# A fifth pair of gates in seven products, block sums in raw tiles of their own, and new deals of the pieces

## The chip, the core and the metric

The kernel runs on one core of one Trainium2 chip. The metric is the device time of one launch in microseconds (us), as the median of several runs. Five engines work side by side: PE (matrix products), DVE and ACT (elementwise work), POOL and SP (here mostly transfers). SP issues nearly all loads of weights. Products are accumulated in PSUM, which has eight banks; everything else lies in SBUF.

## The reference

One decoder block on 256 tokens of width 2048, in float32. Every matrix product below is a float32 product to the accuracy of a split into two parts.

```python
proj = einsum('bsd,de->bse', rmsnorm(x, mix_norm_w), w_in)
(q, k, v, g_out, gk_low, gate_b, gate_c, xc, merge_a, merge_b) = split(proj)
o = rmsnorm(gla_chunked(q, k, v, log_g), gla_norm_w)
y_a = o * silu(g_out)
y_b = gate_b * causal_depthwise_conv(gate_c * xc, conv_w)
merged = sigmoid(merge_a) * y_a + sigmoid(merge_b) * y_b
h = x + merged @ w_out
gu = rmsnorm(h, ffn_norm_w) @ w_gate_up
h = h + (silu(gate) * up) @ w_down
return rmsnorm(h, final_norm_w)
```

## The kernel before

**Pieces.** The weights (some 290 MB) are read once and a little more, in pieces of 128 x 1024 values, 512 KB. A piece goes through four stations: SP issues its load into a buffer `raw`; ACT rounds it into `hi` (`high`, L265); DVE writes the rest into `lo` (`low`, L270); PE multiplies. Each product is three matmuls (`mm3`, L374 to L376): activations hi with weights lo, activations lo with weights hi, hi with hi. There are 5 buffers `raw`, 6 `hi` and 5 `lo`, and `take` loads up to 5 pieces ahead of the one in use. `lo` of a piece is formed one piece later than its `hi` (`halfway`, `finish_low`).

**Eights and sevens.** A group of 512 columns (for instance g3, the third block of `g_out`) is used in one of two ways. As *eights*, it has 8 pieces with 12 matmuls each: two chunks of the contracted dimension, two halves of the tokens. Two groups can also be taken as a *pair in sevens*, by a scheme with seven block products in place of eight: the pair then has 28 pieces of 6 matmuls. In each of four quads q the pieces are `11` (a loaded piece, kept in a buffer y), `t1`, `t3`, `t2`, `t4` (sums of loaded pieces, formed by DVE in `sum_of`), and after the quads come eight pieces `21` and `22`, loaded once more. A pair adds up in five banks, called _0 to _4 after the pair's first key: _0 takes `11` and `21`, _1 takes `t1` and `22`, _2 `t2`, _3 `t3`, _4 `t4`. When the quads are over, DVE combines the banks; bank _1 must be read (`u = pb + v3`) before the `22` pieces may be added on it, and the result goes to a tile that `second` allocates.

**Sums.** `t1` = y + x goes to a `raw` buffer. `t3`, `t2` and `t4` are formed one after the other in place in x, so that each must be split into `hi` and `lo` before the next one overwrites it; `sum_of` calls `finish_low` for that.

**Order of the stream.** `stream_list` writes out the order of all pieces. Between the 28 pieces of a pair it deals eights of other groups, since a piece of a pair gives PE half the work of an eight but DVE as much or more. `GATES` lists the pairs of the gates with the eights mixed into them, `HEADS`, `FIRST`, `dealt` and `GATES_QUADS` say how many eights follow each piece. The program is then given to a scheduler, which sets the order on each engine by its own estimates; each engine works off its list in order.

**Gates.** The pair (gc i, xc i) gives us[i], which the convolution (`conv`, five DVE rows) works on in place; gb i and mb i give sb[i]; g i and ma i give ya[i]. When mb i is done, `merge` multiplies sb[i] by us[i] and adds ya[i], and two transposes on PE bring the result into mh[i], ml[i], which the products of w_out (wo0 to wo3) read. There is one buffer for all us (tag u) and one for all sb, two for ya. Groups in eights use three banks in turn; pairs use the other five, turned by two from pair to pair.

Of the kernel before, what the change touches and what calls it, by code (L numbers as in the profile page):

```python
# [43 lines left out]
def plan():  # L44
# [37 lines left out]
HEADS = (0, 3, 1, 2, 1, 1, 1, 1, 1, 1, 1, 1, 1, 1, 0, 1, 1, 1, 1, 0, 1, 0, 1, 0, 1, 0, 0, 0)  # L82

FIRST = {0: (6, 6, 8, 10, 12), 1: (14, 14, 16, 18, 20), 2: (22, 22, 23, 24, 26), 3: (28, 28, 29, 30, 31)}
FIRST_END = (31, 32)
SEVENS = ((3, 16), (4, 15), (5, 16), (6, 15), (7, 16), (9, 15), (10, 15))

GATES_QUADS = {24: (5, 6, 6, 5)}  # L90
# [20 lines left out]
def dealt(pieces, quads=None):


    out = []
    for n in quads or [(pieces + 3 - q) // 4 for q in range(4)]:
        places = [0] * 5
        for i in (1, 2, 3, 4, 0, 2, 3)[:n]:
            places[i] += 1
        out += places
    rest = pieces - sum(out)  # L120
    return out + [(i + 1) * rest // 8 - i * rest // 8 for i in range(8)]
# [14 lines left out]
def gates_list():  # L136
    out = []
    for pair, keys in GATES:
        eights = [(key, k) for key in keys for k in range(0, KC, 2)]
        out += mixed(pair, eights, dealt(len(eights), GATES_QUADS[len(eights)]) if pair else None)  # L140
    return out


def heads_list():


    step = {"k": 4, "q": 4, "v": 2, "g": 2}
# [16 lines left out]
def hidden_list():  # L164

    plain = []
    for what in PLAIN:
        if isinstance(what, tuple):
            part, fs = what
            plain += [e for n in range(len(DOWN[part])) for f in fs for e in down_of(part, n, f)]  # L170
        else:
            plain += [(f"{name}{what}", k) for name in ("fg", "fu") for k in range(0, KC, 2)]
    plain = [(f"wo{n}", k) for n in range(1, 4) for k in range(0, KC, 2)] + plain

    before = {(what, q): FIRST[q][n] for q in range(4) for n, what in enumerate(("11", "t1", "t3", "t2", "t4"))}
    pair = seven_list(("fg0", "fu0"))
    for n, (_, e) in enumerate(pair[20:]):
        before[e] = FIRST_END[0] + n * (FIRST_END[1] - FIRST_END[0]) // 7
    out, put = [], 0
    for key, e in pair:  # L180
        out += plain[put:before[e]] + [(key, e)]
        put = before[e]
    plain = plain[put:]
    for f, n in SEVENS:
        out += mixed((f"fg{f}", f"fu{f}"), plain[:n], dealt(n))
# [21 lines left out]
def block_kernel(ctx, tc, x, xt, cols_in, gkw_in, gku_in, gnw, conv_w, finw, w_in, w_out, w_gu, w_dn, out):  # L207
# [47 lines left out]

    def fetch(key, k0, pool=wraw, tag="raw"):
        mat, j, n, w = index[(key, k0)]
        raw = pool.tile([P, n, w], F32, tag=tag, name=tag, bufs={"x": 2, "y": 1}.get(tag))
        nc.sync.dma_start(raw, mats[mat][j].rearrange("p (k c) -> p k c", c=w))
        return raw  # L260

# [10 lines left out]
    def sum_of(pair, what, q):  # L272

        one, two = pair
        if what == "21":
            return fetch(one, 4 * q + 2)
        if what == "22":
            return fetch(two, 4 * q + 2)
        if what == "11":
            held["y"] = fetch(one, 4 * q, held["pool"], "y")  # L280
            return held["y"]
        y = held["y"]
        if what == "t1":
            held["x"] = fetch(two, 4 * q, held["pool"], "x")
            raw = wraw.tile([P, 2, 512], F32, tag="raw", name="raw")
            nc.vector.tensor_tensor(out=raw, in0=y, in1=held["x"], op=ALU.add)  # L286
# [5 lines left out]
        nc.vector.tensor_tensor(out=x, in0=x, in1=other, op=ALU.add)  # L292
        return x

    def load_piece():

# [514 lines left out]
    def at(tick, fn):  # L811
        later(tick - count["tick"], fn)
# [142 lines left out]
    class HeadsPool:  # L955
# [62 lines left out]
    def gated(dst, t, ps):  # L1018

        nc.scalar.activation(ps, ps, AF.Sigmoid, scale=r1[:, t:t + 1])  # L1020
        nc.vector.tensor_tensor(out=dst[:, t, :], in0=dst[:, t, :], in1=ps, op=ALU.mult)

    def gate(key):
        i = int(key[-1])

        def done(t, ps):
# [6 lines left out]
            elif key[:-1] == "gb":  # L1033
                if t == 0:
                    sb[i] = ew.tile([P, NT, 512], F32, tag="sb", name="sb")
                nc.scalar.activation(sb[i][:, t, :], ps, AF.Copy, scale=r1[:, t:t + 1])
            elif key[:-1] == "ma":
                gated(ya[i], t, ps)
            else:
                gated(sb[i], t, ps)  # L1040
                if t:

                    at(max(count["tick"] + 1, merge_at.get(i, 0)), lambda: merge(i, slice(0, NT)))

        return done

    def gate_pair(pair):
        i = int(pair[0][-1])

        def second(t):  # L1050
            to = us if pair[0][:-1] == "gc" else sb
            if i not in to:
                to[i] = ew.tile([P, NT, 512], F32, tag="u" if to is us else "sb", name="u" if to is us else "sb")
            return to[i][:, t, :]

        def done(t, one, two):
            if pair[0][:-1] == "gc":
                nc.vector.scalar_tensor_tensor(out=two, in0=one, scalar=r1sq[:, t:t + 1], in1=two,
                                               op0=ALU.mult, op1=ALU.mult)
# [293 lines left out]
```

## Time and profile before

| | |
|---|---|
| time, median of 3 runs | 1500.75 us (1498.3 to 1503.31) |
| span of the profiled execution | 1496.6 us |
| own time of the profiled execution | not listed apart; the three times lie 1.7 to 6.7 us above its span |
| bytes read from HBM | 355.23 MB |
| the slowest engine after PE | DVE |

The page gives, for each engine, the busy time and the number of instructions, then the span in 40 slices with a digit for the busy tenths. Groups of instructions show line, engine, operation, output and inputs, the count, then the busy time with the mean of one in ns, then the engine's idle time ahead of them and what ended it. Rows of waits show who waited for whom: total, times, longest. Matmuls are pipelined: a record lasts longer than the time to the next start, so what a matmul costs is read from start to start.

### The profile page before, as it was taken

How to read it: one execution, taken by the hardware profiler on the slowest of the kernel's cores; microseconds unless marked ns; L12 is line 12 of the kernel's file. 1: busy time of each engine (PE TensorE's matmuls, PEld its weight loads, DVE VectorE, ACT ScalarE, POOL GpSimd, SP SyncE). 2: the span in 40 equal slices, each digit the busy share in tenths (PEclk: the TensorE clock that was granted, in tenths of full speed). 3: DMA queues.
4: the chain of work that ended last, by engine and by line, in shares of the span. 5: the costliest groups of instructions: out<-in, count | busy, mean ns of one | idle time of the engine just before them, and what ended most of it. 6: DMA issues, size and time to landing. Idle time of an engine off the chain costs nothing.

```text
span 1496.6 us, 19397 instructions
## 1 busy us (share of the span) xinstructions
PE 1484.2 (99%) x7040; PEld 1240.5 (83%) x7040; DVE 1308.9 (87%) x1314; ACT 876.6 (59%) x993; POOL 38.9 (3%) x59
## 2 busy tenths in 40 slices
PE   9999999999999999999999999999999999999998
PEld 8989988888888888888888888888888788888887
DVE  7988877879989988876688999999999999999975
ACT  7856565556555654564556756655564556565553
POOL 0030000000001000000000000000000000000000
PEclk9999999999999999999999999999999999999999
DMA  9655677688788888796676777786877778787782
GB/s 351 219 181 185 197 253 230 227 257 277 224 278 259 258 262 247 254 299 212 218 224 211 238 245 248 255 266 221 272 239 240 254 260 274 249 258 235 229 296 96
DMA packets 101280, 362.78 MB, mean 242 GB/s; under 512 B 11620, under 2 KB 11748, under 8 KB 101056
## 3 DMA queue, kind: packets, MB, share of 16 engines
q1 hardware_dynamic: 97808, 350.92, 72.3%
q0 software_dynamic: 2800, 8.89, 2.5%
q10 hardware_dynamic: 576, 1.72, 0.3%
q8 instruction: 55, 0.90, 0.2%
q14 instruction: 41, 0.34, 0.1%
HBM read 355.23 MB, written 2.10 MB: 239 GB/s over the span
## 4 chain that ended last, share of the span: by engine, by line
PE 92%; DVE 3%; issue 1%; ACT 1%; DMA 1%; POOL 1%; SPq 0%; DVEq 0%; ACTq 0%
PE fg L374 8%; PE fg L376 8%; PE fg L375 8%; PE dn L374 5%; PE dn L376 5%; PE dn L375 5%; PE gc L376 3%; PE gc L374 3%; PE gc L375 3%; PE wo L374 2%; PE gb L374 2%; PE wo L375 2%; PE wo L376 2%; PE gb L376 2%; PE ma L374 2%; PE ma L376 2%
## 5 line engine op out<-in xcount | busy, mean ns | idle before, releaser
L270 DVE TENSOR_TENSOR lo<-raw,hi 128x1024 fp32r<-128x1024 f32 (+1 forms) x502 | 606.7, 1216 | 76.8 <-issue 15.7
L265 ACT CAST hi<-raw 128x1024 fp32r<-128x1024 f32 (+1 forms) x502 | 521.0, 1048 | 243.4 <-PE mb L376 29.5
L265 ACT CAST hi<-x 128x1024 fp32r<-128x1024 f32 x156 | 164.3, 1053 | 263.2 <-DVE x L292 198.8
L270 DVE TENSOR_TENSOR lo<-x,hi 128x1024 fp32r<-128x1024 f32 x156 | 190.9, 1224 | 47.5 <-ACT hi L265 27.1
L374 PE MATMUL dn<-lo,acth 128*128 128x512 f32 (+1 forms) x368 | 140.7, 382 | 1.7 <-DVE h L1205 0.9
L376 PE MATMUL dn<-hi,acth 128*128 128x512 f32 (+1 forms) x368 | 139.9, 380 | 0.0
L375 PE MATMUL dn<-hi,actl 128*128 128x512 f32 (+1 forms) x368 | 139.8, 380 | 0.0
L292 DVE TENSOR_TENSOR x<-x,raw 128x1024 f32<-128x1024 f32 x104 | 126.9, 1220 | 12.2 <-DMA raw<-in_w_in_dram 6.6
L374 PE MATMUL fg<-lo,hh 128*128 128x512 f32 x288 | 112.4, 390 | 0.0
L376 PE MATMUL fg<-hi,hh 128*128 128x512 f32 x288 | 112.2, 390 | 0.0
L375 PE MATMUL fg<-hi,hl 128*128 128x512 f32 x288 | 112.1, 389 | 0.0
L374 PE MATMUL fg<-lo,sh 128*128 128x512 f32 x256 | 101.0, 395 | 0.0
L375 PE MATMUL fg<-hi,sl 128*128 128x512 f32 x256 | 99.9, 390 | 0.0
L376 PE MATMUL fg<-hi,sh 128*128 128x512 f32 x256 | 99.8, 390 | 0.0
L374 PEld LDWEIGHTS dn<-lo,acth 128*128 128x128 f32 x368 | 69.2, 188 | 15.8 <-DVE h L1205 1.8
L376 PEld LDWEIGHTS dn<-hi,acth 128*128 128x128 f32 x368 | 69.2, 188 | 13.2
L375 PEld LDWEIGHTS dn<-hi,actl 128*128 128x128 f32 x368 | 69.2, 188 | 13.0
L286 DVE TENSOR_TENSOR raw<-y,x 128x1024 f32<-128x1024 f32 x52 | 64.3, 1236 | 9.2 <-DMA y<-in_w_in_dram 8.2
L270 DVE TENSOR_TENSOR lo<-y,hi 128x1024 fp32r<-128x1024 f32 x52 | 63.5, 1221 | 1.9 <-ACT hi L265 0.8
L292 DVE TENSOR_TENSOR x<-x,y 128x1024 f32<-128x1024 f32 x52 | 63.5, 1221 | 0.7
L374 PEld LDWEIGHTS fg<-lo,hh 128*128 128x128 f32 x288 | 54.1, 188 | 11.8 <-DVE lo L270 0.5
L376 PEld LDWEIGHTS fg<-hi,hh 128*128 128x128 f32 x288 | 54.1, 188 | 11.2
(269 smaller groups left out, 3059.1 us busy)
## 6 DMA issues: line engine op xcount, KB each, us to landing
raw<-in_w_in_dram SPq DMA_DIRECT2D x254, 512.0 KB, 4.6
raw<-in_w_gu_dram SPq DMA_DIRECT2D x176, 512.0 KB, 4.4
raw<-in_w_dn_dram SPq DMA_DIRECT2D x88, 512.0 KB, 4.6
x<-in_w_gu_dram SPq DMA_DIRECT2D x32, 512.0 KB, 5.0
y<-in_w_gu_dram SPq DMA_DIRECT2D x32, 512.0 KB, 4.1
raw<-in_w_out_dram SPq DMA_DIRECT2D x32, 512.0 KB, 4.0
y<-in_w_in_dram SPq DMA_DIRECT2D x20, 512.0 KB, 4.4
x<-in_w_in_dram SPq DMA_DIRECT2D x20, 512.0 KB, 4.4
```

The lines of the kernel that those rows point to most:

```text
L265: nc.scalar.copy(hi[:, ks, :], raw[:, ks, :])
L270: nc.vector.tensor_tensor(out=lo[:, ks, :], in0=raw[:, ks, :], in1=hi[:, ks, :].bitcast(F32), op=ALU.subtract)
L286: nc.vector.tensor_tensor(out=raw, in0=y, in1=held["x"], op=ALU.add)
L292: nc.vector.tensor_tensor(out=x, in0=x, in1=other, op=ALU.add)
L374: nc.tensor.matmul(ps, lhsT=sh, rhs=ml, start=first, stop=False, skip_group_check=onto)
L375: nc.tensor.matmul(ps, lhsT=sl, rhs=mh, start=False, stop=False, skip_group_check=onto)
L376: nc.tensor.matmul(ps, lhsT=sh, rhs=mh, start=False, stop=last, skip_group_check=onto)
```

## The change

It has five parts.

1. `GATES`: g3 and ma3 become a fifth pair, mixed with gb3 and mb3. The eights of the other pairs move: mb1 goes from gc1's to gc2's, gb2 and mb2 are both in gc3's. `second` and `done` learn the new pair: Silu of one sum, Sigmoid of the other, their product, times o[3]. `both` starts the merge of block 3 when the pair and mb3 are done.
2. `sum_of`: t3, t2 and t4 each go to a `raw` buffer of their own; x is held in one buffer instead of two, `raw` has six instead of five. `finish_low` is not called there any more.
3. `DEAL` writes out for each pair how many eights follow each piece; it takes the place of `HEADS`, `FIRST`, `dealt` and `GATES_QUADS`.
4. While the heads run, x and v3 lie in tile m2 and y in m3; v2 alone stays in its pool.
5. `TURN_AT`, `CONV_AT`, `CONV_STEP`: the convolution's five rows and the transposes of some blocks come at other ticks.

```diff
 GATES = (
     (("gc0", "xc0"), ("g1", "gb0", "mb0")),
-    (("gc1", "xc1"), ("ma1", "gb1", "mb1")),
-    (("gc2", "xc2"), ("g2", "ma2", "gb2")),
-    (("gc3", "xc3"), ("mb2", "g3", "ma3")),
-    (None, ("gb3", "mb3")),
+    (("gc1", "xc1"), ("ma1", "gb1")),
+    (("gc2", "xc2"), ("mb1", "g2", "ma2")),
+    (("gc3", "xc3"), ("gb2", "mb2")),
+    (("g3", "ma3"), ("gb3", "mb3")),
 )
...
+LEAD = 6
+SEVENS = (3, 4, 5, 6, 7, 9, 10)
+DEAL = {
+    "v2": "02121 11112 10110 11110 10101010",
...
+    "gc3": "10111 01111 00100 11101 00010110",
+    "g3": "10001 11110 11101 11201 00100000",
+    "fg0": "00312 03222 00132 10101 01000010",
...
+def deal_of(pair):
+
+    return pair and [int(n) for n in DEAL[pair[0]].replace(" ", "")]
...
-    wraw = ctx.enter_context(tc.tile_pool(name="wraw", bufs=5))
+    wraw = ctx.enter_context(tc.tile_pool(name="wraw", bufs=6))
...
         x = held["x"]
-        if halfway and halfway[-1][0] is x:
-            finish_low()
         other = y if what == "t2" else fetch(two if what == "t3" else one, 4 * q + 2)
-        nc.vector.tensor_tensor(out=x, in0=x, in1=other, op=ALU.add)
-        return x
+        raw = wraw.tile([P, 2, 512], F32, tag="raw", name="raw")
+        nc.vector.tensor_tensor(out=raw, in0=x, in1=other, op=ALU.add)
+        held["x"] = raw
+        return raw
...
+    halves_of = {i: 2 if any(pair and pair[0] == f"g{i}" for pair, _ in GATES) else 1 for i in range(4)}
+
+    def both(i):
+
+        halves_of[i] -= 1
+        if not halves_of[i]:
+            at(max(count["tick"] + 1, merge_at.get(i, 0)), lambda: merge(i, slice(0, NT)))
...
+            elif pair[0][:-1] == "g":
+                nc.scalar.activation(one, one, AF.Silu, scale=r1[:, t:t + 1])
+                nc.scalar.activation(two, two, AF.Sigmoid, scale=r1[:, t:t + 1])
+                nc.vector.tensor_tensor(out=two, in0=one, in1=two, op=ALU.mult)
+                nc.vector.tensor_tensor(out=two, in0=two, in1=o[i][:, t, :], op=ALU.mult)
+                if t == 0:
+                    both(i)
...
-TURN_AT = (8, 8, 8, 3)
-CONV_AT = (12, 12, 12, 12)
-CONV_STEP = (1, 1, 1, 1)
+TURN_AT = (8, 7, 10, 3)
+CONV_AT = (12, 12, 14, 12)
+CONV_STEP = (3, 1, 1, 4)
```

The order on the engines, at two places. First the sums on DVE in the last quad of the pair gc3. Before (x and y are the held pieces, `raw` a buffer, numbers tell buffers' uses apart):

```order
L292 TENSOR_TENSOR x_5528<-x_5528,y_5498 128x1024
L270 TENSOR_TENSOR lo_5619<-x_5528,hi_5599 128x1024
L270 TENSOR_TENSOR lo_5632<-raw_5615,hi_5616 128x1024
L292 TENSOR_TENSOR x_5528<-x_5528,raw_5627 128x1024
L270 TENSOR_TENSOR lo_5650<-x_5528,hi_5630 128x1024
```

After:

```order
L287 TENSOR_TENSOR raw_5313<-x_5279,raw_5311 128x1024
L266 TENSOR_TENSOR lo_5317<-raw_5299,hi_5300 128x1024
L287 TENSOR_TENSOR raw_5338<-raw_5313,y_5253 128x1024
L266 TENSOR_TENSOR lo_5329<-raw_5313,hi_5315 128x1024
L266 TENSOR_TENSOR lo_5342<-raw_5325,hi_5326 128x1024
L266 TENSOR_TENSOR lo_5362<-raw_5338,hi_5340 128x1024
```

Before, the `lo` of a sum stands ahead of the next sum, which overwrites x. Now the sum t2 (raw_5338) stands ahead of the `lo` of t3 (lo_5329), and the `lo` rows follow one piece later.

Second the end of gc3 on DVE. Before (v2, v3 are the pair's partial sums, u is us[3]; the merge of block 2, which reads us[2], stands some forty rows ahead):

```order
L452 TENSOR_TENSOR v2_5052<-gc3_2_5049,v2_5052 128x512
L454 TENSOR_TENSOR v3_5690<-gc3_3_5050,v2_5052 128x512
L270 TENSOR_TENSOR lo_5715<-raw_5693,hi_5695 128x1024
L455 TENSOR_TENSOR u_5688<-gc3_1_5048,v3_5690 128x512
L270 TENSOR_TENSOR lo_5729<-raw_5711,hi_5713 128x1024
L459 TENSOR_TENSOR v3_5690<-gc3_4_5051,v3_5690 128x512
```

After, from mb2's last piece (lo_5537) on (lo_5549 is the last "22" piece of gc3, lo_5561 the first of g3, lo_5581 the first of gb3, lo_5595 g3's t1; u_4720 is us[2], u_5430 is us[3]):

```order
L266 TENSOR_TENSOR lo_5537<-raw_5515,hi_5516 128x1024
L266 TENSOR_TENSOR lo_5549<-raw_5533,hi_5535 128x1024
L287 TENSOR_TENSOR raw_5591<-x_5575,raw_5589 128x1024
L266 TENSOR_TENSOR lo_5561<-y_5545,hi_5547 128x1024
L1016 TENSOR_TENSOR sb_5230<-sb_5230,mb2_0_5277 128x512
L1016 TENSOR_TENSOR sb_5230<-sb_5230,mb2_1_5278 128x512
L266 TENSOR_TENSOR lo_5581<-raw_5557,hi_5558 128x1024
L1005 TENSOR_TENSOR sb_5230<-sb_5230,u_4720 128x1024
L287 TENSOR_TENSOR raw_5616<-raw_5591,y_5545 128x1024
L451 TENSOR_TENSOR u_5430<-gc3_1_4948,v3_5432 128x512
L266 TENSOR_TENSOR lo_5595<-raw_5577,hi_5579 128x1024
```

What moved: `u = pb + v3` stood right behind v3; now it stands behind the merge that reads us[2], since both lie in one buffer, and that merge stands behind mb2's last piece.

The same place on PE, one row for each piece or bank (three rows make a product). After:

```order
L370 MATMUL mb2_1_5278<-lo_5537,xh_108 128x512
...
L370 MATMUL g3_0_5643<-lo_5561,xh_108 128x512
...
L370 MATMUL gb3_0_5663<-lo_5581,xh_108 128x512
...
L370 MATMUL gc3_1_4948<-lo_5439,sh_128 128x512
...
L370 MATMUL gc3_1_4948<-lo_5483,sh_128 128x512
...
L370 MATMUL gc3_1_4948<-lo_5519,sh_128 128x512
...
L370 MATMUL gc3_1_4948<-lo_5549,sh_128 128x512
...
L370 MATMUL g3_1_5644<-lo_5595,sh_128 128x512
```

The four "22" pieces of gc3 (bank gc3_1) stood within gc3 before; now they stand behind the first pieces of g3 and gb3. Their `lo` tiles lie in four of the five buffers meanwhile; lo_5537, lo_5561, lo_5581 and lo_5595 have the fifth one in common.

More of the change, by code (lines that the diff above doesn't have):

```diff
@@ L75 @@
     (("gc0", "xc0"), ("g1", "gb0", "mb0")),
-    (("gc1", "xc1"), ("ma1", "gb1", "mb1")),
-    (("gc2", "xc2"), ("g2", "ma2", "gb2")),
-    (("gc3", "xc3"), ("mb2", "g3", "ma3")),
-    (None, ("gb3", "mb3")),
-)
[L82 to L90, printed above, removed]
+    (("gc1", "xc1"), ("ma1", "gb1")),
+    (("gc2", "xc2"), ("mb1", "g2", "ma2")),
+    (("gc3", "xc3"), ("gb2", "mb2")),
+    (("g3", "ma3"), ("gb3", "mb3")),
+)
+LEAD = 6
+SEVENS = (3, 4, 5, 6, 7, 9, 10)
+DEAL = {
+    "v2": "02121 11112 10110 11110 10101010",
+    "gc0": "11111 10111 11211 11121 00110001",
+    "gc1": "01110 11111 01011 01110 00010001",
+    "gc2": "10111 02211 11211 11111 00010101",
+    "gc3": "10111 01111 00100 11101 00010110",
+    "g3": "10001 11110 11101 11201 00100000",
+    "fg0": "00312 03222 00132 10101 01000010",
+    "fg3": "01111 01111 01111 01111 00000000",
+    "fg4": "01111 01111 01111 01110 00000000",
+    "fg5": "00211 01110 01210 10300 00000100",
+    "fg6": "01111 01111 02101 00021 00000000",
+    "fg7": "01111 00111 01211 01111 00000000",
+    "fg9": "01211 00112 00111 01011 00000000",
+    "fg10": "01111 01110 02111 01110 00000000",
+}
 PLAIN = (1, 2, (0, (0, 1, 2)), (1, (3, 4, 5)), 8, (2, (6, 7, 8)))
@@ L108, in seven_list @@
     return [(pair, e) for e in out + list(twos)]
[L111 to L121, printed above, removed]
+def deal_of(pair):
+    return pair and [int(n) for n in DEAL[pair[0]].replace(" ", "")]
 def mixed(pair, eights, gaps):
@@ L139, in gates_list @@
         eights = [(key, k) for key in keys for k in range(0, KC, 2)]
-        out += mixed(pair, eights, dealt(len(eights), GATES_QUADS[len(eights)]) if pair else None)
+        out += mixed(pair, eights, deal_of(pair))
     return out
@@ L173, in hidden_list @@
     plain = [(f"wo{n}", k) for n in range(1, 4) for k in range(0, KC, 2)] + plain
[L175 to L185, printed above, removed]
+    out, plain = plain[:LEAD], plain[LEAD:]
+    for f in (0, *SEVENS):
+        pair = (f"fg{f}", f"fu{f}")
+        n = sum(deal_of(pair))
+        out += mixed(pair, plain[:n], deal_of(pair))
         plain = plain[n:]
@@ L257, in fetch @@
         mat, j, n, w = index[(key, k0)]
-        raw = pool.tile([P, n, w], F32, tag=tag, name=tag, bufs={"x": 2, "y": 1}.get(tag))
+        raw = pool.tile([P, n, w], F32, tag=tag, name=tag, bufs={"x": 1, "y": 1}.get(tag))
         nc.sync.dma_start(raw, mats[mat][j].rearrange("p (k c) -> p k c", c=w))
@@ L961, in tile @@
         def tile(self, shape, dtype, tag, name, bufs=None):
-            if tag not in ("x", "v3"):
+            if tag == "v2":
                 return gpool.tile(shape, dtype, tag=tag, name=name)
-            self.turn += 1
-            return omain.tile(shape, dtype, tag=f"m{2 + self.turn % 2}", name=name)
+            return omain.tile(shape, dtype, tag="m3" if tag == "y" else "m2", name=name)
     held["pool"] = HeadsPool()
@@ L1041, in done @@
                 if t:
-                    at(max(count["tick"] + 1, merge_at.get(i, 0)), lambda: merge(i, slice(0, NT)))
+                    both(i)
         return done
@@ L1050, in second @@
         def second(t):
-            to = us if pair[0][:-1] == "gc" else sb
+            to, tag = {"gc": (us, "u"), "gb": (sb, "sb"), "g": (ya, f"ya{i % 2}")}[pair[0][:-1]]
             if i not in to:
-                to[i] = ew.tile([P, NT, 512], F32, tag="u" if to is us else "sb", name="u" if to is us else "sb")
+                to[i] = ew.tile([P, NT, 512], F32, tag=tag, name=tag)
             return to[i][:, t, :]
@@ L1062, in done @@
                     merge_at[i] = count["tick"] + CONV_AT[i] + 4 * CONV_STEP[i] + 3
+            elif pair[0][:-1] == "g":
[4 more added lines that the diff above has]
+                if t == 0:
+                    both(i)
             else:
```

5 lines of the change are left out of this document (3 added, 2 removed).

## The prediction

> **What bounds the kernel now.** The page comes first, to see which engine is full.
>
> ```profile
> span 1496.6 us, 19397 instructions
> PE 1484.2 (99%) x7040; PEld 1240.5 (83%) x7040; DVE 1308.9 (87%) x1314; ACT 876.6 (59%) x993; POOL 38.9 (3%) x59
> PE   9999999999999999999999999999999999999998
> DVE  7988877879989988876688999999999999999975
> PEclk9999999999999999999999999999999999999999
> PE 92%; DVE 3%; issue 1%; ACT 1%; DMA 1%; POOL 1%; SPq 0%; DVEq 0%; ACTq 0%
> ```
>
> PE is busy in 99% of the span, at full granted clock, and holds 92% of the chain that ended last. So a matmul removed is worth its interval, and a new wait of PE costs its length. The second engine is DVE, at nine tenths in a third of the slices. The waits of PE say how much idle time there is to win back.
>
> ```profile
> PE k L374 <- DVE two L899: 1.3, 1, 1.3
> PE warm_ps L555 <- DVE spare L551: 1.3, 1, 1.3
> PE dn L374 <- DVE h L1205: 0.9, 2, 0.5
> PE dn L374 <- DVE lo L270: 0.8, 1, 0.8
> PE g L374 <- DVE sb L1021: 0.4, 1, 0.4
> PE trb L632 <- DVE sg L1164: 0.2, 1, 0.2
> ```
>
> That is 4.9 us in all, of which 1.3 lie ahead of the first product: at most 3.6 us can be won from waits. Next the price of a matmul, from the timeline of PE near the end of the pair gc2 (start, duration).
>
> ```profile
> 590.82 0.39 PE L376 MATMUL mb<-hi,xh 128*128 128x512 f32 x1
> 591.04 0.39 PE L374 MATMUL g<-lo,xh 128*128 128x512 f32 x1
> ...
> 593.76 0.39 PE L374 MATMUL g<-lo,xh 128*128 128x512 f32 x1
> 594.53 0.50 PE L374 MATMUL g<-lo,xh 128*128 128x512 f32 x1 [0.38 <-DVE sb L1021]
> ```
>
> From 591.04 to 593.76 twelve matmuls start, so one is worth 2.72 / 12 = 0.2267 us, though its record lasts 0.39. The last row is a stall: 0.77 instead of 0.23 from start to start, 0.5 us lost, because a bank of mb2 was still read by DVE. This is the kind of event to look for in the changed program.
>
> **Removed: 24 matmuls.** g3 and ma3 as eights are 16 pieces of 12 matmuls, 192; as a pair in sevens they are 28 pieces of 6, 168. PE's list is shorter by 24 rows, all 512 wide. 24 x 0.2267 = 5.44 us, all on the path: **-5.4**.
>
> **Added on DVE.** Twelve more pieces each need a `lo`, and 16 sums are formed. The groups of DVE (count, busy, mean ns, then idle before them):
>
> ```profile
> L270 DVE TENSOR_TENSOR lo<-raw,hi 128x1024 fp32r<-128x1024 f32 x498 | 603.9, 1221 | 76.2 <-issue 15.7 <-PE gb L374 12.3 <-ACT hi L265 12.2
> L270 DVE TENSOR_TENSOR lo<-x,hi 128x1024 fp32r<-128x1024 f32 x156 | 190.9, 1224 | 47.5 <-ACT hi L265 27.1 <-PE wo L374 4.4 <-PE mb L374 3.2
> L292 DVE TENSOR_TENSOR x<-x,raw 128x1024 f32<-128x1024 f32 x104 | 126.9, 1220 | 12.2 <-DMA raw<-in_w_in_dram 6.6 <-DMA raw<-in_w_gu_dram 5.1
> L1021 DVE TENSOR_TENSOR sb<-sb,mb 128x512 f32<-128x512 f32 x8 | 5.2, 684 | 1.2 <-ACT mb L1020 1.2
> L1058 DVE SCALAR_TENSOR_TENSOR u<-gc,r1sq,u 128x512 f32<-128x512 f32 x4 | 3.0, 746 | 0.0
> ```
>
> A wide row (128x1024) takes 1.22 us, a half one 0.68 to 0.75. The 28 new wide rows are 34 us of DVE, in a stretch that gets shorter. Whether that matters is a sum by stretch. I take it from the first product of gc1 to the end of the last pair of gates, and count rows in the lists of both programs. Before (to the end of gc3): 1368 matmuls of 512 and 24 transposes on PE, 312.1 us of PE's time with a transpose at a third of a matmul; on DVE 156 `lo`, 47 sums, 23 other wide rows and 37 half ones, 226 x 1.22 + 37 x 0.69 = 301.2 us. After (to the end of g3): 1536 matmuls and 24 transposes, 350.2 us; on DVE 184, 61, 27 and 45, so 272 x 1.22 + 45 x 0.69 = 362.9 us. By durations DVE would need 104% of PE's time. But its rows overlap, as its timeline in a full stretch shows:
>
> ```profile
> 589.25 1.22 DVE L292 TENSOR_TENSOR x<-x,raw 128x1024 f32<-128x1024 f32 x1
> 590.39 1.22 DVE L270 TENSOR_TENSOR lo<-raw,hi 128x1024 fp32r<-128x1024 f32 x1
> 591.52 1.22 DVE L1005 TENSOR_TENSOR u<-u,u 128x1024 f32<-128x1024 f32 x1
> 592.66 1.22 DVE L270 TENSOR_TENSOR lo<-x,hi 128x1024 fp32r<-128x1024 f32 x1
> 593.79 1.28 DVE L1021 TENSOR_TENSOR sb<-sb,mb 128x512 f32<-128x512 f32 x2
> ```
>
> Four rows start in 4.54 us, one each 1.135 us, 0.93 of the duration. That gives 280.1 us before (90% of PE's time) and 337.5 after (96%). The windows check the method:
>
> ```profile
> core 0: us, PE busy (x) PEld busy (x) DVE busy (x) ACT busy (x) POOL busy (x), PEclk, DMA share, GB/s
> 320.00:420.00 100.00, 100.00 (x445) 82.52 (x444) 91.28 (x86) 57.28 (x61) 5.01 (x9) 1.00 0.82 255
> 420.00:520.00 100.00, 100.00 (x447) 82.79 (x446) 92.55 (x87) 58.60 (x61) 4.95 (x9) 1.00 0.84 262
> 520.00:620.00 100.00, 99.62 (x444) 82.15 (x443) 89.61 (x83) 54.77 (x57) 4.97 (x9) 1.00 0.80 254
> ```
>
> Their mean is 91.1% of DVE, near the 90% of the sum. So after the change DVE still fits, with 350.2 - 337.5 = 12.7 us to spare in 350, where it had 32 in 312. ACT, at 55 to 59%, hides its 12 more casts; the fifth pair's eight further fetches of 512 KB meet a DMA that is busy to 0.84 at most. Both cost nothing while DVE keeps ahead.
>
> The Trainium skill ("VectorE: DVE Perf Modes", section "The DRAIN you can't avoid") says that the next op does not start until the pipe of the one before is empty, though it allows an earlier start where nothing holds it. By that rule the duration would be the price; the trace's 1.135 against 1.22 speaks against it here.
>
> **Added on PE: the hand-over from gc3 to g3.** Here the new order shows a wait that no trace has. mb2 now ends inside gc3, so us[2] is read late, and us[3], in the same buffer, can only be written after that merge. Until then bank gc3_1 is not free for its four "22" pieces. Their `lo` tiles wait unread in four of five buffers; lo_5537, lo_5561 and lo_5581 go through the fifth one after another. The prices, besides those above, are ACT's cast and sigmoid, and a hand-over from ACT to DVE:
>
> ```profile
> L265 ACT CAST hi<-raw 128x1024 fp32r<-128x1024 f32 (+1 forms) x502 | 521.0, 1048 | 243.4 <-PE mb L376 29.5
> L1020 ACT ACTIVATE mb<-mb,r 128x512 f32<-128x512 f32 x8 | 5.2, 660 | 4.9 <-PE mb L376 4.9
> 605.54 1.05 ACT L265 CAST hi<-x 128x1024 fp32r<-128x1024 f32 x1 [2.69 <-DVE x L292]
> 606.62 1.22 DVE L270 TENSOR_TENSOR lo<-x,hi 128x1024 fp32r<-128x1024 f32 x1 [1.19 <-ACT hi L265]
> ```
>
> The cast ends at 606.59 and DVE starts at 606.62: 0.03 us. Let zero be the time at which PE could start g3's first piece. The last reader of lo_5537 is the third matmul from the end: it starts at -0.68 and ends at -0.29. DVE then writes lo_5561, -0.26 to 0.96; PE goes on at 0.99 (lost: **1.0**). Its six matmuls last to 2.35, their last read of `lo` ends at 2.06. Meanwhile ACT casts hi_5558 after mb2's last matmul (0.19 to 1.24) and takes mb2's second sigmoid (to 1.90); DVE multiplies (1.93 to 2.61) and, overlapping by 0.07, writes lo_5581 (2.54 to 3.76). PE starts gb3 at 3.79 (lost: **1.4**) and ends at 6.51. DVE merges, sums, and forms u_5430 (3.69, 4.83, 5.97, done at 6.65); the "22" pieces start at 6.68 (lost: **0.2**) and run to 12.1. Behind them lo_5655 is done at about 12.5 with 13.5 needed, and g3_3's bank is free at 15.0 with 15.1 needed: nothing more is lost, but DVE has no lead left. Sum **+2.6**. The first two losses follow from one buffer, so the least is 2 x 1.0. For the most, the chain starts late by the two wide rows ahead of lo_5561 (lo_5549, which waits for PE, and raw_5591, which waits for a landing): 2.6 + 2 x 1.135, about 5.
>
> **What else.** The stall of 0.5 us at 594.53 has no successor, as mb2 is followed by other banks: **-0.5**. Behind the hand-over DVE works to just in time for the rest of g3, so one late landing reaches PE there. The waits of DVE in the stretch of before:
>
> ```profile
> DVE lo L270 <- ACT hi L265: 9.1, 16, 1.2
> DVE raw L286 <- DMA y<-in_w_in_dram: 8.2, 3, 3.7
> DVE lo L270 <- issue: 2.0, 4, 0.6
> ```
>
> Three landings of y cost 8.2 us in 312, one in about 100. g3's part is 75 us; I take half of one wait, **+1.4**, between 0 and 3.7. The own raw tiles end a wait of DVE (the `lo` of t3 had to be written ahead of the next sum in place; 27 of the 47.5 us idle before lo<-x are ACT's casts), which is worth nothing while PE does not wait for DVE. They also turn six raw buffers over once a quad, in nine DVE rows or 10 us, where five lasted 1.7 quads; a piece lands in 4.6 us by the page's row below, so I cost this at nothing.
>
> ```profile
> raw<-in_w_in_dram SPq DMA_DIRECT2D x254, 512.0 KB, 4.6
> ```
>
> The new deals leave as many pieces in the hidden part; I cost them at nothing, between -3.6 (all waits of PE gone) and +2. The last matmuls of g3 need DVE and ACT before wo0's second bank is free, but 30 matmuls of wo0's first bank stand between, 6.8 us: hidden.
>
> Sum: -5.4 + 2.6 - 0.5 + 1.4 = -1.9. The profiled execution has a span of 1496.6; the three times lie 1.7 to 6.7 us above it, their median 4.15. The new span would be 1494.7, the time **1498.9 us**, 0.13% less. A measurement can tell some 0.3%, 4.5 us, from no change.
>
> **Rivals.** (1) The waits go too. The hand-over costs only its least, 2.0, nothing is late behind it, and the new deals end the 1.3 us at `two` and the 1.7 at dn: 1500.75 - 5.4 + 2.0 - 0.5 - 3.0 = 1493.8. For it: these waits are single events. Against: `two` waits behind the same pieces of v2 and v3. 0.26. (2) DVE becomes the bound from gc1 to g3. Its waits for ACT, y and issue were 19.3 us in 312, so 21.6 in 350; if they all stay, 21.6 - 12.7 = 8.9 us fall on PE: 1498.9 - 1.4 + 8.9 = 1506.4, slower. It decides where such waits exceed the 12.7 us to spare. For it: eights per seven are fewer in gc1 and gc3. Against: half of these waits are casts that come late because DVE is early. 0.14. (3) DVE's rows do not overlap where they depend on each other: 362.9 - 350.2 = 12.7 us, 1498.9 - 1.4 + 12.7 = 1510.2. The five quoted rows speak against it: 0.03. By the Trainium skill's "VectorE: DVE Perf Modes", section "The DRAIN you can't avoid", this is what would come.
>
> **How the numbers follow.** Forecast 0.57, about 1496.5 to 1502 (hand-over 2.0 to 5, landings 0 to 3.7). Faster by over 0.3%: 0.26, rival 1. Slower: 0.17, rivals 2 and 3. The range runs from 1493.5 to 1504.5: it leaves out the low edge of rival 1, the upper half of rival 2, and rival 3.
>
> **What would show it.** Right: matmuls fewer by 24; in the timeline, PE waits for `lo` twice within 4 us right after mb2's last matmul, then gc3_1 for `u`; DVE at 95 to 98% from there to the end of g3. Wrong: no such wait, then the buffers came free earlier than I read; many short waits of PE for `lo` in gc1 and gc2, then rival 2; a changed interval of matmuls or a clock below 1 would break the whole sum.

## The result, and the profile after

The changed kernel takes 1503.01 us, the median of 22 runs (1500.64 to 1509.39); the kernel before, beside it, 1500.86 (22 runs, 1497.56 to 1504.14). The ratio is 1.0020, with a 95% interval of 1.0013 to 1.0028: slower by 2 to 4 us, where 1.9 us less was forecast. The profiled execution has a span of 1501.3 us, 4.7 more than that of before.

The page of the changed kernel, busy times, slices and the chain that ended last:

```profile
span 1501.3 us, 19356 instructions
PE 1481.7 (99%) x7016; PEld 1238.0 (82%) x7016; DVE 1338.1 (89%) x1348; ACT 893.5 (60%) x1008; POOL 33.0 (2%) x59
DVE  7998877879989998999888998989989999989975
PE 89%; DMA 4%; DVE 4%; issue 2%; ACT 0%; POOL 0%; DVEq 0%; SPq 0%; POOLq 0%; ACTq 0%
```

The 24 matmuls are gone (7040 to 7016), and yet the span is longer. In the chain PE fell from 92 to 89%, and DMA rose from 1 to 4%: landings now stand on the path that sets the end. The waits of PE:

```profile
PE gc L370 <- DVE lo L266: 5.1, 2, 2.7
PE q L370 <- DVE kr L720: 2.2, 1, 2.2
PE warm_ps L551 <- DVE spare L547: 1.3, 1, 1.3
PE gb L370 <- DVE lo L266: 1.0, 1, 1.0
PE g L370 <- DVE lo L266: 0.9, 1, 0.9
PE v L370 <- DVE lo L266: 0.7, 1, 0.7
```

The two rows of 1.0 and 0.9 are the forecast hand-over. The first row is new: two waits in gc pieces, 5.1 us. They stand near 450 us (quad 0 of gc2) and near 589 us (quad 2 to 3 of gc3). What DVE did ahead of the first, by its timeline (start, duration, and idle time before with what ended it):

```profile
441.55 1.22 DVE L287 TENSOR_TENSOR raw<-raw 128x1024 f32<-128x1024 f32 x1
447.22 1.23 DVE L282 TENSOR_TENSOR raw<-y,x 128x1024 f32<-128x1024 f32 x1 [4.46 <-DMA y<-in_w_in_dram]
448.36 2.42 DVE L266 TENSOR_TENSOR lo<-raw,hi 128x1024 fp32r<-128x1024 f32 x2
```

DVE stood 4.46 us at a sum whose y had not landed, and the `lo` tiles that PE needed stand behind that sum in DVE's list. This y was issued by SP at 438.12 and so took 9 us, against a median of 4.8 for y. Its issue, by the timeline of SP:

```profile
438.12 0.33 SPq L255 DMA_DIRECT2D y<-in_w_in_dram  x1
```

And the issues of POOL around it, and ahead of the second stall:

```profile
437.25 0.58 POOL L987 DMA_DIRECT2D u<-u  x1 [38.43 <-DVE u L1060]
...
439.85 0.51 POOL L992 DMA_DIRECT2D u<-u  x1
...
572.96 0.81 POOL L984 DMA_DIRECT2D taps<-in_conv_w_dram  x1 [27.28 <-DVE u L1000]
```

The six shifts of the convolution of block 1 were issued from 437.25 to 439.85, right around it. Later POOL issued the 768 KB of taps, at 572.96, as soon as the last use of the taps before was done. SP's next loads and the sum at which DVE then stood 2.76 us:

```profile
573.83 0.33 SPq L255 DMA_DIRECT2D x<-in_w_in_dram  x1
574.25 0.38 SPq L255 DMA_DIRECT2D raw<-in_w_in_dram  x1
...
584.63 1.22 DVE L287 TENSOR_TENSOR raw<-raw 128x1024 f32<-128x1024 f32 x1 [2.76 <-DMA raw<-in_w_in_dram]
```

The piece that this sum adds was issued at 574.25 and so took 10.4 us. It was also issued late: SP's load ahead of these two stands at 564.21. Since the change there is one buffer for x, which came free with the sum that DVE started at 572.58, and SP's list has the load of x ahead of the others. After such a pause the loads come in a bunch, here together with the taps.

The windows around both stalls (the last three columns are granted clock, DMA share and GB/s):

```profile
438.00:442.00 4.00, 4.00 (x19) 3.30 (x18) 3.96 (x5) 2.01 (x2) 2.36 (x5) 1.00 0.99 292
442.00:446.00 4.00, 4.00 (x20) 3.30 (x19) 0.77 (x1) 1.05 (x1) 0.00 (x0) 1.00 1.01 296
446.00:450.00 4.00, 1.62 (x7) 1.08 (x6) 2.78 (x3) 1.52 (x2) 0.00 (x0) 0.95 1.03 385
450.00:454.00 4.00, 4.00 (x12) 3.14 (x12) 4.00 (x4) 3.31 (x4) 0.00 (x0) 0.63 0.51 177
...
568.00:572.00 4.00, 4.00 (x20) 3.30 (x19) 4.00 (x5) 1.06 (x1) 0.00 (x0) 1.00 0.00 0
...
590.00:594.00 4.00, 4.00 (x13) 3.18 (x12) 4.00 (x4) 1.65 (x3) 0.00 (x0) 0.63 0.33 114
```

The DMA engines are full from 438 to 450, and from 568 to 572 they move nothing. Behind each stall the mean granted clock over 4 us is 0.63, and 12 and 13 matmuls start in them instead of 19 or 20. The trace's record of the clock is sharper: it is one half from 449.6 to 453.0 and from 589.5 to 592.9, 3.4 us each, and full elsewhere from 5.8 to 1497.4. The whole price of a stall is more than its wait. PE's timeline at the first:

```profile
449.64 0.80 PE L370 MATMUL gc<-lo,xh 128*128 128x512 f32 x1 [2.38 <-DVE lo L266]
450.23 0.63 PE L371 MATMUL gc<-hi,xl 128*128 128x512 f32 x1
450.66 0.63 PE L372 MATMUL gc<-hi,xh 128*128 128x512 f32 x1
...
452.79 0.48 PE L371 MATMUL mb<-hi,xl 128*128 128x512 f32 x1
```

From 450.23 to 452.79 seven matmuls start, 0.427 us apart instead of 0.227. Adding up what every start-to-start time has over 0.227 us gives 4.1 us for this stall and 4.5 us for the one near 589. Added up in this way over the whole span, with the matmuls of other widths at their own intervals, the changed kernel has some 10 us more than the kernel before; less 5.4 for the removed matmuls, that is about the 4.7 by which the span grew.

The Trainium skill ("TensorE: Matmul & The Clock Gate", sections "What's actually happening", "Wait — 56ns, not 53.3ns?" and "HAM oscillation — how this bites in real kernels") has half the clock after an idle window of about 3.4 us, and warns of gaps above that. By it a matmul of 512 at half the clock starts every 426.7 ns, and the trace agrees (0.427). But here a wait of 2.38 us was enough; the last section takes this up.

### The profile page after: what moved, and what is told of

It reads as the page before. It is cut to its first block, busy times and chain, and to the rows that moved or that the text cites. A ratio compares the mean times of both kernels' runs of the same rounds, so it can differ in the third digit from the quotient of the medians.

```text
span 1501.3 us, 19356 instructions
## 1 busy us (share of the span) xinstructions
PE 1481.7 (99%) x7016; PEld 1238.0 (82%) x7016; DVE 1338.1 (89%) x1348; ACT 893.5 (60%) x1008; POOL 33.0 (2%) x59
## 4 chain that ended last, share of the span: by engine, by line
PE 89%; DMA 4%; DVE 4%; issue 2%; ACT 0%; POOL 0%; DVEq 0%; SPq 0%; POOLq 0%; ACTq 0%
PE fg L370 8%; PE fg L372 8%; PE fg L371 8%; PE dn L370 5%; PE dn L371 5%; PE dn L372 5%; PE gc L370 3%; PE gc L372 3%; PE gc L371 3%; PE g L372 2%; PE g L371 2%; PE g L370 2%; DVE lo L266 2%; PE mb L370 2%; PE mb L371 2%
## 5 line engine op out<-in xcount | busy, mean ns | idle before, releaser
L261 ACT CAST hi<-raw 128x1024 fp32r<-128x1024 f32 (+1 forms) x666 | 685.9, 1049 | 488.6 <-DVE raw L287 162.8
L266 DVE TENSOR_TENSOR lo<-raw,hi 128x1024 fp32r<-128x1024 f32 (+1 forms) x666 | 797.1, 1217 | 82.7 <-ACT hi L261 26.9
L287 DVE TENSOR_TENSOR raw<-raw 128x1024 f32<-128x1024 f32 x56 | 68.2, 1218 | 12.9 <-DMA raw<-in_w_in_dram 9.6
L287 DVE TENSOR_TENSOR raw<-x,raw 128x1024 f32<-128x1024 f32 x56 | 68.1, 1217 | 11.9 <-DMA raw<-in_w_in_dram 8.3
L282 DVE TENSOR_TENSOR raw<-y,x 128x1024 f32<-128x1024 f32 x56 | 68.2, 1217 | 5.6 <-DMA y<-in_w_in_dram 4.7
L266 DVE TENSOR_TENSOR lo<-y,hi 128x1024 fp32r<-128x1024 f32 x56 | 68.1, 1217 | 2.9 <-PE wo L370 1.0
L287 DVE TENSOR_TENSOR raw<-raw,y 128x1024 f32<-128x1024 f32 x56 | 68.2, 1217 | 0.5
L261 ACT CAST hi<-y 128x1024 fp32r<-128x1024 f32 x56 | 58.8, 1050 | 12.9 <-PE mb L372 3.2
```

The lines of the kernel that those rows point to most:

```text
L261: nc.scalar.copy(hi[:, ks, :], raw[:, ks, :])
L266: nc.vector.tensor_tensor(out=lo[:, ks, :], in0=raw[:, ks, :], in1=hi[:, ks, :].bitcast(F32), op=ALU.subtract)
L287: nc.vector.tensor_tensor(out=raw, in0=x, in1=other, op=ALU.add)
```

## The experiments

Sixteen kernels ran, in four groups. Each was timed beside the kernel before on the same chip; the ratio to it is given with its 95% interval, and 0.001 is 1.5 us. The changed kernel stands at 1.0020. In the expectations theory A is the reading above (two late landings reach PE, because DVE is not far enough ahead of it: it has no lead). By rival B the raw buffers turn over so fast that loads are issued late; by rival C the sum of DVE's work is the bound.

### Group 1: raw tiles, and the transfers

**own_raw**: before, with the sums in raw tiles of their own (`wraw` 6, one `x`) as the only change.

```diff
-        nc.vector.tensor_tensor(out=x, in0=x, in1=other, op=ALU.add)
-        return x
+        raw = wraw.tile([P, 2, 512], F32, tag="raw", name="raw")
+        nc.vector.tensor_tensor(out=raw, in0=x, in1=other, op=ALU.add)
+        held["x"] = raw
+        return raw
```

> The kernel before, with one part of the change alone: each block sum goes into a raw tile of its own (six raw buffers, one x, the heads' x and y as in the change); lists, deals and the pairs of gates stay those of before. Theory A (the change lost because gc1 and gc3 have 16 eights instead of 24, so DVE has no lead there, and two landings of 9 to 10 us, late because the convolution's own shift and taps transfers fill the DMA queues, reach PE): raw tiles alone cost nothing, 1500.9 within 1.5 us of the kernel before, no wait of PE over 2 us. Rival B (the raw buffers turn over once a quad, so fetches are issued late and land late): 3 to 5 us slower than before, about 1504 to 1506, with waits of PE for lo in the pairs of gates. Rival C (DVE's load by itself is the bound): no change, as DVE's rows are as many.

Measured: 1502.86 us, 1.0021 (1.0012 to 1.0031), 3.2 us slower than before. A expected no cost and is wrong here. B's size, 3 to 5 us, fits, but not its place: it expected waits in the pairs of gates, where PE has only one of 0.3 us. The new waits of PE lie in the hidden part (the products of w_out and of the feed-forward):

```profile
PE tr L619 <- DVE h L1097: 3.1, 2, 1.9
...
PE fg L374 <- DVE lo L270: 1.0, 1, 1.0
```

**no_own_raw**: the reverse edit in the changed kernel.

> The changed kernel with the sums formed in place in x again (five raw buffers, two x, the heads' pool as before); lists, deals and the fifth pair stay. Theory A: the two stalls of PE near 450 and 589 us stay or grow, since the late landings and the missing lead are still there: 1502 to 1506. Rival B: both stalls go with the own raw tiles, 8 us less than the changed kernel at most, about 1495 to 1498. Rival C: as the changed kernel, 1503 within 1.5.

Measured: 1512.64 us, 1.0086 (1.0073 to 1.0099). In-place sums make it 10 us worse, which is against B; but A's range, 1502 to 1506, is missed too, and its stalls do not stay or grow. In this trace the gc pieces wait 1.7 us in three times, at most 0.7, and waits of PE up to 2.5 us stand at other places. So in the changed lists the raw tiles are worth 10 us, where in the lists of before they cost 3.2; and the run does not clear late issue of a part in the two stalls.

**after_no_conv_dma** and **before_no_conv_dma**: both kernels without the shifts, and with one load of taps in place of four.

```diff
-        nc.gpsimd.dma_start(taps, conv_w[:, :, i * 512:(i + 1) * 512].to_broadcast([P, 3, 512]))
...
-        nc.gpsimd.dma_start(u1[1:113, :, :], u[0:112, :, :])
-        nc.gpsimd.dma_start(u2[2:114, :, :], u[0:112, :, :])
...
-        for n, (dst, src, by, op) in enumerate(((u1, u1, 1, ALU.mult), (u2, u2, 0, ALU.mult), (u, u, 2, ALU.mult),
+        for n, (dst, src, by, op) in enumerate(((u1, u, 1, ALU.mult), (u2, u, 0, ALU.mult), (u, u, 2, ALU.mult),
```

> The changed kernel without the convolution's shift transfers and without three of its four loads of taps (the products take u unshifted and block 0's taps, so the output is another); arithmetic rows, lists and deals stay. Theory A: without these transfers y and raw land in 4 to 5 us, the stalls near 450 and 589 us (wait and slow clock behind them, 4.1 + 4.5 us over the interval) go: 6 to 8.6 us less than the changed kernel, 1494.5 to 1497. Rival B: landings are late because they are issued late, so at most 2 us less, 1501 to 1503. Rival C: no change, 1503 within 1.5.

> The kernel before without the same transfers (same products left out). Theory A: in the kernel before the same late landings (y in 6.6 to 8.5 us) were covered by DVE's lead, so taking them away is worth nothing: 1500.9 within 1.5. Rival B and C: nothing as well. If it is 4 us or more faster, the transfers cost PE in both kernels alike and can't tell the two apart.

Measured: 1495.3 us, 0.9975 (0.9965 to 0.9985), 6.8 us less than the changed kernel by the ratios; and 1499.24 us, 0.9996 (0.9988 to 1.0005), nothing. The waits of PE in the gates, 355 to 704 us, of the changed kernel without them:

```profile
PE gb L370 <- DVE lo L266: 1.0, 1, 1.0
PE g L370 <- DVE lo L266: 0.9, 1, 0.9
PE trb L628 <- DVE ml L631: 0.3, 1, 0.3
```

Both stalls are gone and the hand-over is left. So the same transfers cost 6.8 us after the change and nothing before it that can be told from noise (1.5 us). Late issue alone makes no stall: SP pauses as long in this trace, from 560.07 to 569.15, and the loads of x and raw issued then land in time.

### Group 2: one part of the change at a time

**no_fifth**: the changed kernel with the four pairs of before, 24 eights in each in the regular deal of before, and the convolution's and transposes' ticks of before. The edit of the pairs:

```diff
-    (("gc3", "xc3"), ("gb2", "mb2")),
-    (("g3", "ma3"), ("gb3", "mb3")),
+    (("gc3", "xc3"), ("mb2", "g3", "ma3")),
+    (None, ("gb3", "mb3")),
```

> The changed kernel without its fifth pair: own raw tiles and the new deals of the heads and of the hidden part stay, g3 and ma3 are eights again, four pairs of gates with 24 eights each in the regular deal of before, and the convolution's and turns' times of before. 24 matmuls more (+5.4). Theory A: with 24 eights per pair DVE has its lead again, so both stalls (4.1 + 4.5 over the interval) and the hand-over (2.2) go: 1503.0 + 5.4 - 10.8 = 1497.6 within 2. If the loss came from the raw tiles or the new deals instead, the stalls stay: 1503.0 + 5.4 - 2.2 = 1506.

Measured: 1497.71 us, 0.9976 (0.9967 to 0.9985). With 24 matmuls more it is 6.6 us faster than the changed kernel, and faster than before. What DVE waited for from 355 to 704 us, here and in the changed kernel:

```profile
DVE lo L266 <- PE gb L370: 13.3, 10, 1.5
DVE lo L266 <- PE mb L370: 6.4, 6, 1.5
...
DVE lo L266 <- PE ma L370: 5.4, 5, 1.4
```

```profile
DVE lo L266 <- ACT hi L261: 5.7, 9, 1.2
DVE raw L282 <- DMA y<-in_w_in_dram: 4.7, 2, 4.5
DVE raw L287 <- DMA raw<-in_w_in_dram: 3.5, 3, 2.8
DVE v L448 <- PE gc L372: 3.1, 2, 1.7
```

This is how lead is read. A `lo` that waits for PE waits for a free buffer: DVE has then filled all five, and a late landing uses up that lead before PE stands. no_fifth has over 25 us of such waits, the changed kernel has none.

**old_v2**: the changed kernel with the heads' deal of v2 and v3 of before.

> The changed kernel with the deal of v2 and v3 in the heads as before; the rest stays. The heads' new deal has waits of 0.9 and 2.35 us of PE (v for lo, q for kr) where before had one of 1.8 (k for two). If the deal makes them: 1 to 1.5 us less than the changed kernel, 1501.5 to 1502, wait for kr gone. If the waits come from the own raw tiles in the heads (x and y in other buffers): no change, 1503 within 1.

Measured: 1502.05 us, 1.0012 (1.0003 to 1.0021): 1.2 less, the bounds overlap. The wait for kr is gone, one for `two` of 1.7 us is back.

**spread**: the transfers of the convolution in series.

```diff
+        nc.gpsimd.dma_start(u2[1:113, :, :], u1[0:112, :, :])
...
+        nc.gpsimd.tensor_tensor(out=taps[:, 0, 0:64], in0=u2[:, 0, 0:64], in1=u2[:, 0, 0:64], op=ALU.add)
         nc.gpsimd.dma_start(taps, conv_w[:, :, i * 512:(i + 1) * 512].to_broadcast([P, 3, 512]))
...
-        nc.gpsimd.dma_start(u2[2:114, :, :], u[0:112, :, :])
```

> The changed kernel with the convolution's transfers one after the other instead of at once: u1 is shifted from u, u2 is shifted from u1 (so it waits until u1 has landed), and the taps are issued after u2 has landed instead of as soon as their buffer is free. Same bytes, same arithmetic. Theory A (two stalls of PE near 450 and 589 us from landings of 9 to 10 us beside these transfers): both stalls shrink or go, 4 to 8 us less than the changed kernel, 1495 to 1499. If it is the bytes and not their crowding, the late landings only move elsewhere: 1501 to 1505, with stalls of PE at other places of the gates. Rival C (DVE's load alone): 1503 within 1.5.

Measured: 1515.83 us, 1.0092 (1.0072 to 1.0113). A miss, and a poor test: the taps now land after the products that use them, and DVE waits for those.

```profile
DVE u L1001 <- DMA taps<-in_conv_w_dram: 19.2, 4, 6.5
```

**free_u**: the last sum of the convolution goes to u1, which frees the buffer that the hand-over waits for.

```diff
+        us[i] = u1
...
-                                                (u1, u1, u2, ALU.add), (u, u, u1, ALU.add))):
+                                                (u1, u1, u2, ALU.add), (u1, u, u1, ALU.add))):
```

> The changed kernel with the convolution's last sum written to u1 instead of u, so that the buffer of u is free for the next pair's result without waiting for the merge. Same arithmetic. The prediction's hand-over from gc3 to g3 (PE waits of 1.08 and 1.14 us near 624 to 627, because us[3] shares its buffer with us[2], which the merge reads late): if that buffer is the cause, both waits go and 1.5 to 2.2 us are saved, 1501 within 1; if the cause is the one lo buffer whatever u does, no change, 1503. The two stalls at 450 and 589 stay in either case.

Measured: 1506.19 us, 1.0028 (1.0016 to 1.0040): not faster, though both waits of the hand-over are gone from the trace. Group 4 takes this up.

### Group 3: lead and crowding by other means

**even**: five pairs, with 20, 20, 20, 20 and 16 eights. **even_v2**: the same with the old deal of v2.

```diff
-    "gc1": "01110 11111 01011 01110 00010001",
+    "gc1": "01111 11111 01111 01111 00010101",
```

> The changed kernel, fifth pair kept, with the 96 eights dealt as 20, 20, 20, 20, 16 over the pairs gc0, gc1, gc2, gc3 and g3 (16 in each quad part 4 to 5 at a time, 3 in the tail) instead of 24, 16, 24, 16, 16; keys run over the ends of pairs; matmuls, DVE rows and transfers are as many. Theory A (late landings reach PE only where DVE has no lead, in the pairs with 16 eights): the stalls of gc2's start and of gc3 shrink by most of their 8.6 us; the hand-over to g3 stays: 1495 to 1498. If the late landings alone decide and lead does not matter, or if DVE's load over the whole stretch is the bound: 1502 to 1505, the stalls elsewhere.

> As even, with the deal of v2 and v3 of before in the heads too. If theory A holds for even, this is 0.5 to 1.5 us less than even, 1494 to 1497, and the fastest version; if the lead does not matter, 1501 to 1504.

Measured: 1510.13 us, 1.0064 (1.0052 to 1.0077), and 1509.74, 1.0059 (1.0047 to 1.0071). Both miss. This deal makes waits of its own, in the same view of PE:

```profile
PE gb L372 <- DVE ya L1018: 3.8, 2, 2.3
PE g L372 <- DVE sb L1018: 1.6, 1, 1.6
```

PE waits there for banks that DVE has yet to read. Where the eights stand matters besides how many they are, so these two do not test lead by itself.

**spread_late**: spread, with the products five ticks later (`CONV_AT = (17, 17, 19, 17)`).

> The transfers one after the other, as in spread (there the taps landed after the products that use them, and DVE waited 19.2 us for them in four times), with the convolution's products five ticks later in each pair. Theory A: DVE no longer waits for taps, and as in spread no stall of PE over 1 us stands at 450 and at 589: 1496 to 1500. If crowding is not the cause, the stalls come up elsewhere in gc1 to gc3: 1502 to 1506.

Measured: 1511.51 us, 1.0072 (1.0059 to 1.0085). A miss for both. DVE's wait for taps is down to 2.1 us, but PE waits more often in gc and mb pieces (9 times, 8.9 us, longest 1.8). Moving the transfers in time did not help; only leaving them out did. So it is not shown that their crowding is what makes landings late, and not their bytes.

**no_fifth_v2**: no_fifth with the old deal of v2: own raw tiles and the hidden part's deals alone.

> The changed kernel without its fifth pair, and with the deal of v2 and v3 of before: what is left of the change is the own raw tiles and the deals of the hidden part. The heads' new deal was worth about -1 us against (old_v2, 0.9 less than the changed kernel, with bounds that overlap): 1496.7 if that holds, 1497.7 if it makes no difference. Own raw tiles alone were 3.3 us slower than before, so the deals of the hidden part would be worth some 6 us.

Measured: 1495.52 us, 0.9968 (0.9956 to 0.9980): the fastest complete kernel, 4.8 us below before.

### Group 4: which transfer, whose lead, and the hand-over

**no_taps**: one load of taps for all blocks. **no_shifts**: no shifts, all taps.

> The changed kernel with block 0's taps loaded once and used for all four blocks (the output is another); the shift transfers stay. If the stall near 589 is made by the load of the taps issued at 573, it goes (4.5 us) and the one near 450, behind the shifts issued at 437 to 440, stays: 1503.0 - 4.5 = 1498.5 within 1.5. If both stalls are the shifts' or neither's: 1502 to 1504.

> The changed kernel without the shift transfers (the products take u unshifted, so the output is another); all four loads of taps stay. If the stall near 450 is made by the shifts, it goes (4.1 us) and the one near 589 stays: 1503.0 - 4.1 = 1498.9 within 1.5. If both stalls are the taps': both stay, 1502 to 1504.

Measured: 1501.88 us, 1.0011 (1.0002 to 1.0020), and 1497.82 us, 0.9984 (0.9975 to 0.9993). The traces agree with the expectations. Without taps one wait in gc pieces is left, near 449; without shifts one near 582, of 1.3 us:

```profile
PE gc L370 <- DVE lo L266: 2.7, 1, 2.7
```

```profile
PE gc L370 <- DVE lo L266: 1.3, 1, 1.3
```

In time the shifts are worth 5.4 us, as expected within its bound. The taps are worth 1.4, a third of what the profiled execution had suggested, and with bounds that overlap those of the changed kernel. Together that is 6.8, as in after_no_conv_dma.

**few_rows**: all transfers, but four of the five DVE rows of each convolution left out.

> The changed kernel with all transfers, but with four of the five DVE rows of each convolution left out (only u times its third tap stays, so the output is another). Three to four of these rows of 1.14 us lie in gc3 between 567 and 578, right ahead of the stall near 589; those of gc2 lie behind the stall near 450. If the missing lead of DVE is half of the cause, the stall near 589 goes or falls below 1 us and that near 450 stays about as it is: 1503.0 - 4.5 = 1498.5 within 2. If the late landing alone decides, both stay: 1502 to 1503.

Measured: 1505.05 us, 1.0033 (1.0020 to 1.0045). In its trace PE's wait near 589 fell from 2.7 to 1.3 us and that near 450 stayed at 2.4, as expected of lead; the clock stayed full behind both. But the time did not fall. Taps are free earlier there and their load moves, DVE's waits for raw grow (13.8 us from 312 to 760, against 7.5), and the hand-over takes 2.8 us. So it cannot tell lead from landing.

**free_u_no_dma**: free_u and no transfers.

> free_u (the last sum in u1, so the buffer of u comes free) and no transfers of the convolution, both (the output is another). after_no_conv_dma was 1495.3 with the two hand-over waits (2.2 us) as its only stalls in the gates. If the hand-over costs what it shows: 1493.2 within 1. If DVE sets the pace from gc3 to g3, so that PE waits as long at another place: 1495 to 1496, with waits for lo or u behind 628.

Measured: 1496.36 us, 0.9973 (0.9962 to 0.9983); after_no_conv_dma had 0.9975. The waits of PE from 541 to 760 us with free_u:

```profile
PE mb L370 <- DVE lo L266: 0.9, 2, 0.6
PE g L370 <- DVE u L1056: 0.6, 1, 0.6
PE g L370 <- DVE lo L266: 0.4, 2, 0.3
```

That is 1.9 us, as the 1.0 + 0.9 of the hand-over that they replace. So from gc3 to g3's end DVE sets the pace: the kernel's time did not fall when these two waits of PE were taken away.

## Why the prediction was wrong, point by point

- **24 matmuls, -5.4.** The count is right, and where the clock is full the interval is 0.227 as before.
- **Hand-over, +2.6.** The mechanism and its two first waits came as told: PE stopped 1.08 us ahead of g3 and 1.14 us ahead of gb3 over the interval, by the chain of `lo` tiles through one buffer; 1.0 and 1.4 were forecast.

```profile
622.66 0.39 PE L372 MATMUL mb<-hi,xh 128*128 128x512 f32 x1
623.97 0.50 PE L370 MATMUL g<-lo,xh 128*128 128x512 f32 x1 [0.92 <-DVE lo L266]
...
625.24 0.40 PE L372 MATMUL g<-hi,xh 128*128 128x512 f32 x1
626.60 0.51 PE L370 MATMUL gb<-lo,xh 128*128 128x512 f32 x1 [0.97 <-DVE lo L266]
```

  The third wait, 0.2 for `u`, did not come. Measured 2.2. What the term missed is that the two waits are a symptom: without them PE waits as long elsewhere.
- **The stall at 594.53, -0.5.** Gone, as told.
- **One late landing, +1.4: the step that failed.** It was placed behind the hand-over, half a wait of y long, at most 3.7. It came twice, at gc2's start and in gc3, and cost 4.1 and 4.5 us in the profiled execution. Three things made it so large. First, "Both cost nothing while DVE keeps ahead" was taken from a sum over the whole stretch, 337.5 of 350.2 us, 96%. Counted in the same way by pair (44 wide rows of the pair, 7 others, one for each eight, 11 half rows): with 24 eights 75 x 1.135 + 11 x 0.64 = 92.2 us of DVE in 456 x 0.2267 + 0.5 = 103.9 us of PE, 89%; with 16 eights 67 x 1.135 + 7.0 = 83.0 in 360 x 0.2267 + 0.5 = 82.1, 101%. What there is to spare lies in gc2 alone, 11.7 us by this count; gc1, gc3 and g3 have none. The profiles agree where PE hardly stops: from 355 to 437 us, most of gc1, DVE (third column) is busy 74.10 of 82 us before the change, 90%, and 80.25 behind it, 98%.

```profile
355.00:437.00 82.00, 82.00 (x366) 67.61 (x365) 74.10 (x68) 44.27 (x47) 1.84 (x3) 1.00 0.83 255
355.00:437.00 82.00, 81.67 (x364) 67.05 (x363) 80.25 (x77) 46.74 (x49) 2.26 (x4) 1.00 0.74 253
```

  Second, the sum knows a landing by its median; beside the convolution's transfers the two loads took 9.0 and 10.4 us, and without these transfers both stalls are gone and 6.8 us with them. Third, the price of a stall was its wait; here the clock fell behind it, some 1.7 us more each time. The prediction named a clock below 1 as what would break its sum, and gave it no chance.
- **Own raw tiles and new deals, at nothing.** Both are large, with opposite signs. From the ratios: raw tiles alone +3.2 us; the deals of the hidden part with them -4.8 in all, so the deals some -8; the heads' deal +1.2 (0.9968 to 0.9976, and the same from old_v2, each with bounds that overlap); the fifth pair +6.6. The fifth pair stands here for all that no_fifth takes back, its deals and ticks too. The sum is the +3.0 of the changed kernel, as it must be, since each step is the difference of two runs. The prediction had costed the turnover of six raw buffers at nothing because a piece lands in 4.6 us; the landings of 9.0 and 10.4 us end that reason. How much of the two stalls is late issue stays open: with five raw buffers and two for x they shrink to at most 0.7 us a wait, in a kernel that is 10 us slower for other waits.
- **The rivals.** Rival 2, DVE as the bound from gc1 to g3, was closest in sign and place, with 0.14; its time, 1506.4, was 3.4 us too high. Its mechanism was only half of it: it expected many short waits; there were two long ones and the hand-over. Rival 1 is out, as the waits grew. So is rival 3: back to back, a wide row still starts 1.14 us after the one ahead of it, as at 447.22 and 448.36.

What is shown: with the deals and ticks that come with it, the fifth pair costs 6.6 us net of its 24 matmuls; and without the convolution's transfers the changed kernel gets 6.8 us back and the kernel before none. That missing lead is what lets the late landings through is read from the traces, not shown by a run of its own. For it: in the kernel before, DVE stood 3.73 us for a y, up to 569.95, and PE did not wait for any `lo` from 355 to 704 us; in the changed kernel 4.46 us of DVE cost PE 2.38, and no `lo` ever waits there for a free buffer. What stays open: whether five pairs can be dealt so that DVE has lead, as even and few_rows brought disturbances of their own; how much the late issue behind the one buffer of x adds; and why the taps are worth less in the median than in the profile, though the profiled execution of no_taps, at 1499.7 us, was the second lowest of its eleven.

## What to carry to other kernels

When a change takes work from the engine that bounds the kernel, add up the next engine's load for each stage, not for the stretch: 96% was 89% in one pair and 101% in three. Lead can be read before the change, as the time that the second engine waits for the first to free a buffer; where it goes to zero, a late landing can reach the path. And a change in several parts should be tried in parts: two of these together gained 4.8 us, and the one that gave the change its name lost more than that.

## What was not expected of the hardware

- Behind a wait of 2.38 us the granted clock was one half for 3.4 us, but not behind one of 2.79 us, in old_v2 at the same place:

```profile
448.27 0.50 PE L370 MATMUL gc<-lo,xh 128*128 128x512 f32 x1 [2.79 <-DVE lo L266]
...
449.99 0.39 PE L371 MATMUL mb<-hi,xl 128*128 128x512 f32 x1
```

  From 448.60 on, its matmuls are 0.23 us apart. The traces' records of the granted clock say when it falls. Within each of the eighteen traces its changes lie a multiple of 3.413 us apart (in the changed kernel 449.56 and 589.51, 41 steps), and each of the fourteen stretches at half the clock inside a kernel lasts one such step. Counted by the starts of matmuls, a transpose at a third of one, PE was at work in at most 36% of the step just ahead of each of them, and in at least 41% of every step that none followed. In the changed kernel the step from 446.1 to 449.6 holds nearly the whole wait, and PE works in 28% of it. In old_v2 a step ends at 447.0, within the wait; 50% and 60% are left on its two sides. So the wait alone does not decide, but how it lies to these steps, whose first one starts at another time in each trace, 4.4 to 7.1 us into the span.

  The Trainium skill ("TensorE: Matmul & The Clock Gate", section "What's actually happening") has such a window of 3413 ns, which runs freely; the traces agree with both.
- Beside the convolution's shifts a 512 KB landing took 9 us instead of 4.8, at a DMA share of 0.99 to 1.03.
